# Two projections of a transformer layer in column blocks of 512 instead of 256, and a residual formed one stage earlier

## The chip, the core and the metric

The kernel runs on one core of a Trainium2 chip. The metric is the device time of one execution in microseconds (us). The core's engines work side by side, each through its own queue of instructions: TensorE (PE in the profile; its weight loads are PEld), VectorE (DVE), ScalarE (ACT), GpSimd (POOL) and SyncE (SP, which here only issues transfers). On-chip data lies in SBUF, results of TensorE in PSUM, which has eight banks of 128 x 512 fp32 here.

## What is computed

One layer of a token mixer with a feed-forward part, 1024 tokens of width 1024. Only the second half of it is touched:

```python
mix = (sigmoid(gate_a) * y_m + sigmoid(gate_b) * y_g) @ w_out      # output projection, 1024 x 1024
h = layer_norm(ALPHA * h + g1 * mix, ln1_g, ln1_b)
gate, val = split((h * (1 + sc2) + sh2) @ w_up + b_up)              # up projection, 1024 x 5632
f = (gelu(conv3x3(gate) + conv_b) * val) @ w_down + b_down          # down projection, 2816 x 1024
h = layer_norm(ALPHA * h + g2 * f, ln2_g, ln2_b)
```

The first half (two kinds of recurrent attention, their gates and their branch projections) is the same in both kernels. All is fp32. The kernel splits each operand of these products into a high and a low part (`hi` rounded to the matmul's type, `lo = x - hi`) and forms hi·hi + hi·lo + lo·hi, three matmuls for each 128 rows of the contraction.

## The kernel before

`layer_kernel` is one long function. A framework takes the instructions in program order, tracks which tiles each reads and writes, sets all waits, and may issue an instruction earlier than its place if its tiles are free; on each queue the order is then fixed, and a waiting instruction holds those behind it. Tiles with one tag share `bufs` buffers and rotate.

**Weights.** `wload` (L255) loads a piece of 2 x 128 rows by 256 columns (256 KB) through SyncE into `raw` (4 buffers), and `split` (L251) makes `hi` on ScalarE (L252) and `lo` on VectorE or GpSimd (L253), into the ring `whi`/`wlo` (6 buffers each) or into tiles given as `into`. `mm3` (L279) runs the three matmuls over all k (L283 to L285).

**SBUF places.** `slot(i)` are 16 tiles of 4 KB a partition, `ubt(i)` are 20 (`u0` to `u19`). The branch projections read slots 0 to 15 (`s` in the profile) until their last matmul, then the pool of the slots is closed and opened anew (L999 to L1001).

**Output projection** (L1041 to L1086). Token tiles 0 to 3 (`th` 0) and then 4 to 7, each in four blocks of 256 columns (`cb_`), in the order 2, 0, 1, 3 and 3, 0, 1, 2. The weights of blocks 2 and 3 go through the ring, those of 0 and 1 into slots where they stay for both halves. `mix` (L1046) loads the token tile of x once (`nt`, L1049), runs 24 matmuls of 256 columns into a `pj` bank (there are 2), multiplies by the gate row (L1055), adds ALPHA x (L1056) and takes partial statistics (L1057). In a half's last block `norm1` (L1059) normalizes the tile and stores it to DRAM as `n_d`. `mod2` (L1064) transposes four normalized tiles on TensorE, scales them on ScalarE into `u` (L1072, 3 buffers), and splits them (L1074 on VectorE, L1075 on GpSimd and VectorE in turn) into the slots that the up projection reads; the half 0 is done within the output projection, the half 1 in the first round of the up projection (L1107).

**Up projection** (L1092 to L1130). 22 rounds, each with 128 gate and 128 value columns: four groups of 24 matmuls of 512, copies out on ScalarE (L1105), a 3 x 3 convolution as eight operations on VectorE (L1120), gelu on ScalarE (L1123), the product with the value (L1124). Rounds 0 to 9 are split into `u0` to `u19` (ScalarE and GpSimd), rounds 10 to 21 are stored to DRAM as `gl_d`.

**Down projection** (L1134 to L1243). The contraction is cut in two: `g` 0 is rounds 0 to 9, `g` 1 rounds 10 to 21. For each of four blocks of 256 columns all eight token tiles have a result bank at once (`bt`: all eight banks of PSUM), and the loop takes a piece of two k at a time, all eight tiles for each. `ahead(i + 5)` keeps the ring loaded. At the end of a block VectorE forms z = result x g2 (L1201). For `g` 0 the residual is formed here: SyncE reloads `n_d` by block into `y` (L1189), VectorE multiplies and adds two rows (`gab`, `bab`, L1190 and L1191), adds z (L1203), and SyncE stores the sum to `b1_d` (L1204). During `g` 0, `reload` (L1137) brings rounds 10 to 21 back and splits them on GpSimd (L1143, L1144). Then `nt` takes the residual from `b1_d`, and for `g` 1 `evac2` (L1160) adds z and takes statistics (L1163). The last two blocks of `g` 1 run tile by tile instead (L1228), each tile 2 x 12 x 3 matmuls followed by its statistics, normalization and output store; six pieces of their weights go into other tiles (`late`, `wlate`).

Of the kernel before, what the change touches and what calls it, by code (L numbers as in the profile page):

```python
# [15 lines left out]
P = 128  # L16
# [20 lines left out]
def layer_kernel(ctx, tc, I, out, dbg=None):  # L37
# [995 lines left out]
    bst = cst.tile([P, 8, 4, 6], F32, name="bst")  # L1033
# [3 lines left out]
    def stats(t):  # L1037
# [3 lines left out]
    wo = I["w_out"]  # L1041
    wres = [([slot(4, [P, 4, 256], F32R), slot(5, [P, 4, 256], F32R)], [slot(12, [P, 4, 256], F32R), slot(13, [P, 4, 256], F32R)]),
            ([slot(6, [P, 4, 256], F32R), slot(7, [P, 4, 256], F32R)], [slot(14, [P, 4, 256], F32R), slot(15, [P, 4, 256], F32R)])]
    wb, nt, uhi, ulo = {}, {}, {}, {}

    def mix(t, cb_):  # L1046
        if t not in nt:
            nt[t] = lp.tile([P, D], F32, tag=f"n{t}", name=f"n{t}") if t < 5 else ubt(12 + t, [P, D])
            SY.dma_start(nt[t][:], x[t * P:(t + 1) * P, :])  # L1049
# [5 lines left out]
        V.tensor_tensor(m[:], p[:], g1b[:, s_], op=ALU.mult)  # L1055
        V.scalar_tensor_tensor(y, y, ALPHA, m[:], op0=ALU.mult, op1=ALU.add)  # L1056
        V.bn_stats(bst[:, t, cb_, :], y)  # L1057
# [6 lines left out]
    def mod2(th):  # L1064
        uhi[th] = [slot(4 * th + i, [P, 2, 512], F32R) for i in range(4)]
        ulo[th] = [slot(8 + 4 * th + i, [P, 2, 512], F32R) for i in range(4)]
        for k in range(KD):
# [3 lines left out]
            u = lp.tile([P, 512], F32, tag="u", name=nm("u"), bufs=3)  # L1071
# [4 lines left out]

    for th in range(2):
        for cb_ in ((2, 0, 1, 3), (3, 0, 1, 2))[th]:
            if th == 0 or cb_ == 2:
                wb[cb_] = wload([(wo, cb_ * 256, 256, 0)], into=wres[cb_] if cb_ < 2 else None)  # L1080
            for t in range(4 * th, 4 * th + 4):
                mix(t, cb_)
                if cb_ == 3 - th:
                    norm1(t)
            if th == 1 and cb_ == 3:
# [4 lines left out]
    gl_d = [drt(f"gl{f}", [P, SEQ]) for f in range(N_RES, NF)]  # L1090
    glu = {}
    for f in range(NF):  # L1092
# [7 lines left out]
        for b in range(2):  # L1100
# [23 lines left out]
        V.tensor_tensor(val[:], val[:], af, op=ALU.mult)  # L1124
        if f < N_RES:
# [9 lines left out]
    b1_d = [drt(f"b1{t}", [P, D]) for t in range(8)]  # L1135

    def reload(f):  # L1137
        t = fin.tile([P, SEQ], F32, tag="gl", name=nm("gl"), bufs=2)
        G.dma_start(t[:], gl_d[f - N_RES][:])
# [3 lines left out]
        G.tensor_scalar(hi[:], t[:], 1.0, None, op0=ALU.mult)  # L1143
        G.tensor_tensor(lo[:], t[:], hi[:].bitcast(F32), op=ALU.subtract)  # L1144
# [3 lines left out]
    todo = [(g, cb_, k) for g, (k0, k1) in enumerate(((0, N_RES), (N_RES, NF))) for cb_ in range(4)  # L1148
            for k in range(k0, k1, 2)]
    late = todo[-(NF - N_RES) // 2:]  # L1150
    wch = {}

    def prod(p, t, kk, w, first, last):
        lh, ll = (a[:, t * P:(t + 1) * P] for a in glu[kk])
        rh, rl = w(kk % 2, 0, 256)
        T.matmul(p[:], lh, rh, start=first, stop=False)  # L1156
        T.matmul(p[:], lh, rl, start=False, stop=False)  # L1157
        T.matmul(p[:], ll, rh, start=False, stop=last)  # L1158

    def evac2(t, cb_, z):  # L1160
        y = nt[t][:, cb_ * 256:cb_ * 256 + 256]
        V.tensor_tensor(y, y, z[:], op=ALU.add)
        V.bn_stats(bst[:, t, cb_, :], y)  # L1163
# [10 lines left out]
    for i, c in enumerate(todo):  # L1174
        g, cb_, k = c
        k0, k1 = ((0, N_RES), (N_RES, NF))[g]
        s_ = slice(cb_ * 256, cb_ * 256 + 256)
        if k == k0:
            acc = [pt(b, [P, 256]) for b in bt]
            if g == 0:  # L1180
                gab = fin.tile([P, 256], F32, tag="gab", name=nm("gab"), bufs=2)
                bab = fin.tile([P, 256], F32, tag="bab", name=nm("bab"), bufs=2)
                rowb(gab[:], fr_d[0:1, s_])
                rowb(bab[:], fr_d[1:2, s_])
        if g == 0 and k == k0 + 2:
            y4 = [fin.tile([P, 4, 256], F32, tag="y", name=nm("y"), bufs=2) for _ in range(2)]
            ys = [y4[t // 4][:, t % 4, :] for t in range(8)]
            for t, y in enumerate(ys):
                SY.dma_start(y, n_d[t][:, s_])  # L1189
                V.tensor_tensor(y, y, gab[:], op=ALU.mult)  # L1190
                V.tensor_tensor(y, y, bab[:], op=ALU.add)  # L1191
        if c[:2] in ((1, 2), (1, 3)):
            break
        ahead(i + 5)
        for t in range(8):
            for kk in (k, k + 1):
                prod(acc[t], t, kk, wch[c], kk == k0, kk == k1 - 1)
            if k + 2 < k1:
                continue
            z = fin.tile([P, 256], F32, tag="z", name=nm("z"), bufs=4)  # L1200
            V.tensor_tensor(z[:], acc[t][:], g2b[:, s_], op=ALU.mult)  # L1201
# [66 lines left out]
```

## Time and profile before

| | us |
|---|---|
| median of 3 runs | 2344.84 (2343.28 to 2349.64) |
| the profiled execution's own time | 2350.07 |
| its span, first to last instruction | 2348.3 |
| PE busy in it | 2265.5 (96%) |
| VectorE busy | 1363.5 (58%) |
| ScalarE busy | 719.4 (31%) |
| output projection, from 1488.9 to 1597.3 | 108.4 |
| down projection's matmuls, from 2072.4 to 2338.7 | 266.3 |

Times in the profile count from the span's start. A row of a timeline gives the start, the duration, the engine (an ending q means its queue, where a transfer is issued), the line, the operation, output and inputs, the count of merged instructions, and in brackets the idle time before it with what ended that. L283 to L285 are `mm3`'s matmuls, L1156 to L1158 those of the down projection. A matmul's row names the output bank, then the streamed operand, then the stationary one. Matmuls overlap, so a row's duration is longer than its share of time. In a group's row, count and shape come first, then busy us, mean ns, and the idle time before with what ended it.

### The profile page before, as it was taken

To read this page: it belongs to the slowest core of one execution; us is meant where nothing else is said; L and a number is where in the kernel's file an instruction comes from. 1 tells how busy PE (TensorE), PEld (TensorE's weight loads), DVE (VectorE), ACT (ScalarE), POOL (GpSimd) and SP (SyncE) were. 2 spreads that over 40 slices of the span, in tenths; PEclk is the share of its full clock that TensorE was granted. 3 is DMA by queue.
4 is the path that set the end of the run, shared out by engine and by line. 5 is a ranking of instruction groups with operands and counts; after the bars stand their busy time and mean duration, and the time that the engine had idled before them with its cause. 6 is when DMAs were issued, how large, how long until landed. Compare 5 with 4: busy or idle time off the path is not lost. (4 is left out here: it accounts for less than half of the span.)

```text
span 2348.3 us, 33481 instructions
## 1 busy us (share of the span) xinstructions
PE 2265.5 (96%) x13081; PEld 1965.0 (84%) x13081; DVE 1363.5 (58%) x2695; ACT 719.4 (31%) x1231; POOL 301.1 (13%) x254
## 2 busy tenths in 40 slices
PE   8989999998999999998999999999999999989998
PEld 4979898987889888897877788997888888889998
DVE  6484736475564645655345543577566556567457
ACT  3563323324332322313431143214333333311110
POOL 1010101111110111101210032101110000034300
PEclk9999999999999999999999999999999999999999
DMA  8222121203441333323357544512111122245511
GB/s 280 80 103 75 41 65 46 61 17 105 108 112 53 104 86 99 99 81 110 97 167 232 186 147 139 175 64 81 37 53 54 61 74 72 77 135 186 196 55 64
DMA packets 200848, 239.42 MB, mean 102 GB/s; under 512 B 16801, under 2 KB 155681, under 8 KB 200689
## 3 DMA queue, kind: packets, MB, share of 16 engines
q1 hardware_dynamic: 183521, 188.61, 25.8%
q0 software_dynamic: 8960, 31.63, 5.2%
q10 hardware_dynamic: 8208, 17.04, 2.0%
q8 instruction: 103, 1.69, 0.3%
q14 instruction: 56, 0.46, 0.1%
HBM read 183.42 MB, written 45.41 MB: 97 GB/s over the span
## 5 line engine op out<-in xcount | busy, mean ns | idle before, releaser
L252 ACT ACTIVATE whi<-raw 128x512 fp32r<-128x512 f32 x314 | 197.3, 630 | 516.1 <-PE pj L285 214.5
L283 PE MATMUL pj<-u,whi 128*128 128x512 f32 (+1 forms) x816 | 317.3, 389 | 20.3 <-DVE s L743 8.5
L253 DVE TENSOR_TENSOR wlo<-raw,whi 128x512 fp32r<-128x512 f32 x314 | 229.5, 735 | 157.5 <-ACT whi L252 153.4
L284 PE MATMUL pj<-u,whi 128*128 128x512 f32 (+1 forms) x816 | 314.3, 385 | 0.0
L285 PE MATMUL pj<-u,wlo 128*128 128x512 f32 (+1 forms) x816 | 313.8, 385 | 0.0
L283 PE MATMUL pj<-s,whi 128*128 128x512 f32 x784 | 305.6, 390 | 0.0
L285 PE MATMUL pj<-s,wlo 128*128 128x512 f32 x784 | 305.4, 390 | 0.0
L1120 DVE SCALAR_TENSOR_TENSOR acc<-g,colF,acc 128x945 f32<-128x945 f32 (+2 forms) x168 | 205.0, 1220 | 155.7 <-ACT acc L1111 153.6
L284 PE MATMUL pj<-s,whi 128*128 128x512 f32 x744 | 290.1, 390 | 2.3 <-POOL s L1075 2.3
L283 PE MATMUL pj<-whi,u 128*128 128x256 f32 x768 | 218.0, 284 | 0.0
L285 PE MATMUL pj<-whi,u 128*128 128x256 f32 x768 | 217.6, 283 | 0.0
L284 PE MATMUL pj<-wlo,u 128*128 128x256 f32 x768 | 217.6, 283 | 0.0
L283 PEld LDWEIGHTS pj<-u,whi 128*128 128x128 f32 x816 | 156.1, 191 | 51.2 <-ACT s L769 14.6
L285 PEld LDWEIGHTS pj<-u,wlo 128*128 128x128 f32 x816 | 156.0, 191 | 26.7
L284 PEld LDWEIGHTS pj<-u,whi 128*128 128x128 f32 x816 | 156.3, 192 | 25.9
L283 PEld LDWEIGHTS pj<-s,whi 128*128 128x128 f32 x784 | 147.2, 188 | 30.9
L285 PEld LDWEIGHTS pj<-s,wlo 128*128 128x128 f32 x784 | 147.2, 188 | 30.8
L284 PEld LDWEIGHTS pj<-s,whi 128*128 128x128 f32 x744 | 139.7, 188 | 33.0 <-POOL s L1075 3.6
L283 PEld LDWEIGHTS pj<-whi,u 128*128 128x128 f32 x768 | 147.4, 192 | 0.5
L284 PEld LDWEIGHTS pj<-wlo,u 128*128 128x128 f32 x768 | 147.4, 192 | 0.0
L285 PEld LDWEIGHTS pj<-whi,u 128*128 128x128 f32 x768 | 147.4, 192 | 0.0
L727 DVE SCALAR_TENSOR_TENSOR s<-pj,colB,s 128x511 f32<-128x511 f32 (+2 forms) x96 | 57.5, 613 | 92.2 <-ACT s L732 91.3
(486 smaller groups left out, 4479.8 us busy)
## 6 DMA issues: line engine op xcount, KB each, us to landing
u<-in_w_mod_dram SPq DMA_DIRECT2D x48, 512.0 KB
raw<-in_w_in_dram SPq DMA_DIRECT2D x96, 256.0 KB
raw<-in_w_up_dram SPq DMA_DIRECT2D x176, 128.0 KB
raw<-in_w_in_dram SPq DMA_DIRECT2D x96, 128.0 KB
raw<-in_w_down_dram SPq DMA_DIRECT2D x44, 256.0 KB
s<-rmask POOLq DMA_DIRECT2D x16, 512.0 KB, 5.2
s<-rr POOLq DMA_DIRECT2D x16, 512.0 KB, 7.9
qq<-re POOLq DMA_DIRECT2D x16, 512.0 KB, 6.5
```

Source lines behind the costliest of these rows:

```text
L252: A.activation(hi, src, AF.Copy)
L253: eng.tensor_tensor(lo, src, hi.bitcast(F32), op=ALU.subtract)
L283: T.matmul(p, lh, rh, start=k == 0, stop=False)
L284: T.matmul(p, lh, rl, start=False, stop=False)
L285: T.matmul(p, ll, rh, start=False, stop=k == nk - 1)
L727: V.scalar_tensor_tensor(y[:, o:o + src.shape[1]], src, t, y[:, o:o + src.shape[1]], op0=ALU.mult, op1=ALU.add)
L1120: V.scalar_tensor_tensor(av, g[:, r0 + dy:r1 + dy, c0 + dx:c1 + dx], convw(3 * ky + kx, f), av, op0=ALU.mult, op1=ALU.add)
```

## The change

Output projection: two blocks of 512 columns instead of four of 256, in the order 0, 1 and 1, 0, both blocks' weights in slots (block 0 in 4 to 7 and 12 to 15, block 1 in 0 to 3 and 8 to 11). A piece is now one k by 512 columns (`wload1`), the same 256 KB. Tiles `m` are twice as wide, `u` has two buffers instead of three, statistics have two parts a tile.

Up projection: in rounds 1 to 4, two token tiles each, GpSimd's queue loads `n_d`, VectorE multiplies and adds the two rows over all 1024 columns, and GpSimd's queue stores the result as `y_d`.

Down projection: two blocks of 512 columns, one k a step, the last two k of a block in one step per tile; eight result tiles as before. For `g` 0 only z is formed and stored to `z_d` through ScalarE's queue. The residual is put together by two transfers, `z_d` into `nt` and `y_d` added to it by an accumulating transfer on GpSimd's queue, one tile a step in the first eight steps of `g` 1. Rounds 10 to 21 are split on ScalarE and VectorE. Only the last block of `g` 1 runs tile by tile.

```diff
+    def wload1(src, c0, k, into=None):
+        raw = stg.tile([P, 512], F32, tag="raw", name=nm("raw"), bufs=4)
+        SY.dma_start(raw[:], src[k * P:(k + 1) * P, c0:c0 + 512])
+        if into is None:
+            into = [stg.tile([P, 512], F32R, tag=t, name=nm(t), bufs=6)[:] for t in ("whi", "wlo")]
+        split(into[0], into[1], raw[:], V)
+        return into
...
+    wres = {0: (4, 12), 1: (0, 8)}
...
+    def wout(cb_):
+        hs = [[slot(s0 + i, [P, 2, 512], F32R) for i in range(4)] for s0 in wres[cb_]]
+        wb[cb_] = [wload1(I["w_out"], cb_ * 512, k, [h[k // 2][:, k % 2, :] for h in hs]) for k in range(KD)]
...
-        p = pt("pj", [P, 256])
+        p = pt("pj", [P, 512])
...
-            u = lp.tile([P, 512], F32, tag="u", name=nm("u"), bufs=3)
+            u = lp.tile([P, 512], F32, tag="u", name=nm("u"), bufs=2)
...
+    wout(0)
     for th in range(2):
-        for cb_ in ((2, 0, 1, 3), (3, 0, 1, 2))[th]:
-            if th == 0 or cb_ == 2:
-                wb[cb_] = wload([(wo, cb_ * 256, 256, 0)], into=wres[cb_] if cb_ < 2 else None)
+        for cb_ in (th, 1 - th):
+            if th == 0 and cb_ == 1:
+                wout(1)
...
+        if f == 1:
+            gab, bab = ubt(16, [P, D]), ubt(17, [P, D])
+            rowb(gab[:], fr_d[0:1, :])
+            rowb(bab[:], fr_d[1:2, :])
+        if 1 <= f <= 4:
+            ys = [ubt(18 + i, [P, D]) for i in range(2)]
+            for i, y in enumerate(ys):
+                G.dma_start(y[:], n_d[2 * f - 2 + i][:])
...
+        if 1 <= f <= 4:
+            for i, y in enumerate(ys):
+                V.tensor_tensor(y[:], y[:], gab[:], op=ALU.mult)
+                V.tensor_tensor(y[:], y[:], bab[:], op=ALU.add)
+                G.dma_start(y_d[2 * f - 2 + i][:], y[:])
...
-        G.tensor_scalar(hi[:], t[:], 1.0, None, op0=ALU.mult)
-        G.tensor_tensor(lo[:], t[:], hi[:].bitcast(F32), op=ALU.subtract)
+        split(hi[:], lo[:], t[:], V)
...
-            wch[c] = wload([(I["w_down"], c[1] * 256, 256, 0)], nk=2, k0=c[2], eng=V)
+            wch[c] = wload1(I["w_down"], c[1] * 512, c[2])
...
+    loads = dict(zip((0, 2, 4, 6, 8, 10, 12, 14, 15, 16, 17, 18), range(N_RES, NF)))
+    splits = dict(zip((2, 4, 6, 8, 10, 12, 14, 16, 17, 18, 20, 21), range(N_RES, NF)))
+    main = todo[:-(NF - N_RES)]
+    for i, (g, cb_, k) in enumerate(main):
...
+            acc = [pt(b, [P, 512]) for b in bt]
+        ahead(i + 6)
+        if k == k1 - 1:
+            continue
+        ks = (k, k + 1) if k == k1 - 2 else (k,)
+        for t in range(8):
+            for kk in ks:
+                prod(acc[t], t, kk, wch[(g, cb_, kk)], kk == k0, kk == k1 - 1)
+            if len(ks) == 1:
+                continue
+            z = scaled(acc[t], s_, t % 2 if g == 0 else 0)
             if g == 0:
...
-                V.tensor_tensor(ys[t], z[:], ys[t], op=ALU.add)
-                SY.dma_start(b1_d[t][:, s_], ys[t])
-                continue
-            evac2(t, cb_, z)
+                A.dma_start(z_d[t][:, s_], z[:])
+            else:
+                evac2(t, cb_, z)
+        if i in splits:
+            gsplit(splits[i])
+        if i in loads:
+            gload(loads[i])
...
+        if i < 28:
+            t = i - 20
+            nt[t] = ubt(12 + t, [P, D])
+            SY.dma_start(nt[t][:], z_d[t][:])
+            G.dma_start(nt[t][:], y_d[t][:], accum_op=ALU.add)
...
+    for j, c in enumerate(todo[len(main):]):
+        if j >= 6:
+            if j < 10:
+                h = (ubt(10 + j - 6, [P, 2, 512], F32R) if j < 8 else
+                     fin.tile([P, 2, 512], F32R, tag="gl", name=nm("wlate"), bufs=2))
+                h = [h[:, 0, :], h[:, 1, :]]
+            else:
+                h = [fin.tile([P, 512], F32R, tag="z1", name=nm("wlate"), bufs=4)[:] for _ in range(2)]
+            wch[c] = wload1(I["w_down"], c[1] * 512, c[2], h)
+        elif c not in wch:
+            wch[c] = wload1(I["w_down"], c[1] * 512, c[2])
     for t in range(8):
-        for cb_ in (2, 3):
+        for cb_ in (1,):
...
+            evac2(t, cb_, scaled(p, slice(cb_ * 512, cb_ * 512 + 512)))
```

More of the change, by code (lines that the diff above doesn't have):

```diff
@@ L1032, in layer_kernel @@
     n_d = [drt(f"n{t}", [P, D]) for t in range(8)]
-    bst = cst.tile([P, 8, 4, 6], F32, name="bst")
+    bst = cst.tile([P, 8, 2, 6], F32, name="bst")
     mv = cst.tile([P, 8, 2], F32, name="mv")
@@ L1090, in layer_kernel @@
     gl_d = [drt(f"gl{f}", [P, SEQ]) for f in range(N_RES, NF)]
+    y_d = [drt(f"y{t}", [P, D]) for t in range(8)]
     glu = {}
@@ L1134, in layer_kernel, with gload, gsplit @@
     fin = ctx.enter_context(tc.tile_pool(name="fin", bufs=1))
[L1135 to L1139, printed above, removed]
+    z_d = [drt(f"z{t}", [P, D]) for t in range(8)]
+    gt, yt = {}, {}
+    def gload(f):
+        gt[f] = fin.tile([P, SEQ], F32, tag="gl", name=nm("gl"), bufs=2)
+        G.dma_start(gt[f][:], gl_d[f - N_RES][:])
+    def gsplit(f):
+        t = gt[f]
         i = 2 * (f - N_RES)
@@ L1154, in prod @@
         lh, ll = (a[:, t * P:(t + 1) * P] for a in glu[kk])
[L1155 to L1163, printed above, removed]
+        T.matmul(p[:], lh, w[0], start=first, stop=False)
+        T.matmul(p[:], lh, w[1], start=False, stop=False)
+        T.matmul(p[:], ll, w[0], start=False, stop=last)
     def ahead(i):
@@ L1167, in ahead, with scaled, evac2 @@
             c = todo[len(wch)]
-            wch[c] = wload([(I["w_down"], c[1] * 256, 256, 0)], nk=2, k0=c[2], eng=V)
+            wch[c] = wload1(I["w_down"], c[1] * 512, c[2])
+    def scaled(p, s_, i=0):
+        z = fin.tile([P, 512], F32, tag=f"z{i}", name=nm("z"), bufs=4)
+        V.tensor_tensor(z[:], p[:], g2b[:, s_], op=ALU.mult)
+        return z
+    def evac2(t, cb_, z):
+        y = nt[t][:, cb_ * 512:cb_ * 512 + 512]
+        V.tensor_tensor(y, y, z[:], op=ALU.add)
+        V.bn_stats(bst[:, t, cb_, :], y)
     g2b = fin.tile([P, D], F32, name="g2b")
@@ L1178, in layer_kernel @@
         if k == k0:
-            acc = [pt(b, [P, 256]) for b in bt]
-            if g == 0:
[L1181 to L1191, printed above, removed]
@@ L1207, in layer_kernel @@
-        if g == 0:
-            if i % 2 == 1 and i < 16:
-                reload(N_RES + i // 2)
-            if cb_ == 3 and k in (0, 2):
-                reload(N_RES + 8 + k)
-                reload(N_RES + 9 + k)
-            if i == 4 * (N_RES // 2) - 1:
-                lgb, lbb = ubt(8, [P, D]), ubt(9, [P, D])
-                rowb(lgb[:], I["ln2_g"].unsqueeze(0))
-                rowb(lbb[:], I["ln2_b"].unsqueeze(0))
-                for t in range(8):
-                    nt[t] = ubt(12 + t, [P, D])
-                    SY.dma_start(nt[t][:], b1_d[t][:])
@@ L1222, in layer_kernel @@
-    ahead(len(todo) - len(late))
-    for c in late:
-        j = late.index(c)
-        h = (ubt(10 + j, [P, 2, 2, 256], F32R) if j < 2 else
-             fin.tile([P, 2, 2, 256], F32R, tag=("gl", "y")[j // 2 - 1], name=nm("wlate"), bufs=2))
-        wch[c] = wload([(I["w_down"], c[1] * 256, 256, 0)], nk=2, k0=c[2], eng=V, into=([h[:, 0]], [h[:, 1]]))
+            acc = [pt(b, [P, 512]) for b in bt]
[3 more added lines that the diff above has]
+        ks = (k, k + 1) if k == k1 - 2 else (k,)
@@ L1228, in layer_kernel @@
     for t in range(8):
-        for cb_ in (2, 3):
-            bank = (2 * t + cb_) % 4
-            p = pt(("pj", "pa", "po", "pt")[bank], [P, 256])
+        for cb_ in (1,):
+            p = pt(("pj", "pa", "po", "pt")[t % 4], [P, 512])
             for kk in range(N_RES, NF):
-                prod(p, t, kk, wch[(1, cb_, kk - kk % 2)], kk == N_RES, kk == NF - 1)
-            z = fin.tile([P, 256], F32, tag="z", name=nm("z"), bufs=4)
-            V.tensor_tensor(z[:], p[:], g2b[:, cb_ * 256:cb_ * 256 + 256], op=ALU.mult)
-            evac2(t, cb_, z)
+                prod(p, t, kk, wch[(1, cb_, kk)], kk == N_RES, kk == NF - 1)
+            evac2(t, cb_, scaled(p, slice(cb_ * 512, cb_ * 512 + 512)))
```

38 lines of the change are left out of this document (13 added, 25 removed).

## Prediction

> **What bounds the kernel now.** First the page, for which engine the time belongs to, and what one matmul seems to cost; its columns are count, busy us, mean ns.
>
> ```profile
> span 2348.3 us, 33481 instructions
> ...
> L283 PE MATMUL pj<-s,whi 128*128 128x512 f32 x784 | 305.6, 390 | 0.0
> ...
> L283 PE MATMUL pj<-whi,u 128*128 128x256 f32 x768 | 218.0, 284 | 0.0
> ```
>
> The means mislead: 284 against 390 ns would make two matmuls of 256 columns 178 ns dearer than one of 512. Matmuls overlap, so what one costs is the stretch divided by the count. The table of stretches gives both (stretch; length; PE, PEld, DVE, ACT, POOL busy; granted clock; DMA share; GB/s):
>
> ```profile
> 1488.90:1597.30 108.40, 106.79 (x850) 104.70 (x850) 79.72 (x213) 20.46 (x32) 7.07 (x5) 1.00 0.38 129
> 1610.00:2072.40 462.40, 462.40 (x2041) 383.01 (x2040) 277.50 (x277) 169.28 (x226) 23.92 (x10) 1.00 0.20 61
> 2072.40:2101.50 29.10, 29.09 (x241) 28.80 (x240) 15.94 (x18) 4.80 (x7) 8.63 (x5) 1.00 0.60 189
> 2101.50:2108.80 7.30, 0.15 (x2) 0.00 (x0) 7.30 (x13) 0.63 (x1) 6.58 (x5) 0.67 0.49 144
> 2108.80:2116.00 7.20, 6.68 (x29) 6.38 (x30) 7.20 (x13) 0.00 (x0) 7.09 (x5) 0.50 0.40 127
> 2118.50:2272.00 153.50, 153.44 (x1276) 153.24 (x1277) 88.30 (x173) 20.84 (x33) 45.78 (x22) 1.00 0.49 158
> 2272.00:2338.70 66.70, 66.65 (x556) 66.44 (x554) 51.24 (x138) 0.00 (x0) 0.00 (x0) 1.00 0.15 56
> 2338.70:2348.30 9.60, 0.00 (x0) 0.00 (x0) 5.49 (x15) 0.00 (x0) 0.00 (x0) 0.72 0.15 55
> ```
>
> The up projection (1610 to 2072, all 512 wide) takes 462.4/2041 = 0.2266 us a matmul; the down projection's undisturbed end (256 wide) takes 66.7/556 = 0.120. So two narrow ones cost 0.2400 and one wide 0.2266: 13.4 ns a pair. TensorE is never idle in these stretches, so it sets the time there; PE is idle in one place only, 2101.5 to 2108.8, and at half clock after it. The timeline of PE and the chain that ended last say why:
>
> ```profile
> 1557.92 0.39 PE L283 MATMUL pj<-s,u 128*128 128x256 f32 x1 [1.61 <-DVE m L1055]
> ```
> ```profile
> 2108.83 0.58 PE L1156 MATMUL pj<-whi,u 128*128 128x256 f32 x1 [7.18 <-DVE z L1201]
> ```
> ```profile
> 2090.47 6.83 DMA y<-n
> 2097.30 2.14 DVE y L1190
> ```
>
> VectorE waited for the residual's reload, so its product z, which frees the result bank, came late.
>
> **The change, part by part.** Counts come from the loops. Output projection: 8 token tiles x 4 blocks x 24 = 768 matmuls become 384: 384 x 13.4 ns = 5.1 us. Down projection: 22 x 4 x 8 x 3 = 2112 become 1056: 14.2 us. Both lie wholly on PE, the path: **19.3 us gained**.
>
> [...]
>
> The reload's wait. 2072.4 to 2338.7 is 266.3 us; 2112 x 0.120 = 253.4; the excess is **12.9 us**, of it 7.2 us idle, 0.5 in a second gap that I leave in the sum, the rest half clock. The change takes residual work out of this stage (it is formed in rounds 1 to 4 of the up projection), and also Pool's splitting, so z is a single operation per tile; all 12.9 goes. In the output projection the 1.61 us wait (1.8 with its restart) goes too: a bank is now filled in 5.4 us instead of 2.9, so VectorE has longer. Gains together: **34.0 us**.
>
> The residual in the up projection adds two tiles x two operations a round:
>
> ```profile
> 2038.81 1.23 DVE L1124 TENSOR_TENSOR val<-val,acc 128x1024 f32<-128x1024 f32 x1 [1.19 <-ACT acc L1123]
> 2047.44 1.20 DVE L1120 SCALAR_TENSOR_TENSOR acc<-g,colF,acc 128x945 f32<-128x945 f32 x1 [7.40 <-ACT acc L1111]
> ...
> 2053.79 0.69 DVE L253 TENSOR_TENSOR wlo<-raw,whi 128x512 fp32r<-128x512 f32 x1
> ```
> ```profile
> L253 POOL TENSOR_TENSOR u<-val,u 128x1024 fp32r<-128x1024 f32 x9 | 21.5, 2393 | 173.0 <-ACT u L252 173.0
> ...
> L252 ACT ACTIVATE u<-val 128x1024 fp32r<-128x1024 f32 x9 | 9.5, 1060 | 12.1 <-DVE val L1124 12.1
> ```
> ```profile
> L1190 DVE TENSOR_TENSOR y<-y,gab x32: 410/418/3047, 2097.3 to 2182.7; 128x256 f32<-128x256 f32 x32
> ```
> ```profile
> DMA to landing us min/median/max: 3.8/4.7/9.0
> ```
>
> 4 x 1.23 = 4.9 us; between one round's product and the next convolution VectorE idles 7.40 us, which hides them. Pool's split falls into the same gap, and the y row shows an operation stretched from 0.42 to 3.05 us beside Pool; 4.9 + 2.39 = 7.3 just fits. If the cover is gone PE feels it: a round is 96 x 0.2266 = 21.75 us, round 21 starts at 2050.65 and needs the last weight difference after 19 matmuls, at 2054.95, and it ends at 2054.48. So 0.5 us is the slack. Cost 0; other end 4 x 2.4 = 9.6. The two reads and two writes a round are Pool's, where only that split waits behind them; the last row is Pool's reload of 512 KB later in the kernel, 4.7 us. The two broadcasts in round 1 stand on SyncE's queue until the second modulation has read the tiles they overwrite, some 10 us; the weight loads behind them are for round 2, 21.75 us off.
>
> The output projection's start is the first new wait. Its first block went into the ring, ahead of time; now it goes into slots that the branch projection reads until its last matmul.
>
> ```profile
> 1489.11 0.39 PE L283 MATMUL pj<-whi,u 128*128 128x256 f32 x1
> ```
> ```profile
> 1482.00 0.63 ACT L993 ACTIVATE gt<-gt 128x512 f32<-128x512 f32 x1 [2.02 <-DMA gt<-tha]
> ...
> 1489.05 1.67 ACT L252 ACTIVATE s<-raw 128x512 fp32r<-128x512 f32 x3 [2.40 <-PE pa L285]
> ...
> 1500.73 2.80 ACT L252 ACTIVATE s<-raw 128x512 fp32r<-128x512 f32 x4 [8.97 <-DMA raw<-in_w_out_dram]
> ```
> ```profile
> 1490.34 2.98 DVE L253 TENSOR_TENSOR s<-raw,s 128x512 fp32r<-128x512 f32 x3
> ...
> 1496.01 0.42 DVE L1056 SCALAR_TENSOR_TENSOR n<-n,m 128x256 f32<-128x256 f32 x1 [1.76 <-DMA n<-in_x_dram]
> ...
> 1497.45 0.42 DVE L1056 SCALAR_TENSOR_TENSOR n<-n,m 128x256 f32<-128x256 f32 x1 [0.23 <-DMA n<-in_x_dram]
> ```
> ```profile
> 1479.35 0.32 SPq L992 DMA_DIRECT2D gt<-tha  x1
> ...
> 1489.21 0.34 SPq L1049 DMA_DIRECT2D u<-in_x_dram  x1
> 1490.44 1.77 SPq L1049 DMA_DIRECT2D n<-in_x_dram  x4
> 1492.32 3.46 SPq L263 DMA_DIRECT2D raw<-in_w_out_dram  x4
> ```
>
> Slots open at 1489.05. The raw ring holds four of eight pieces; VectorE needs 1 us each from 1490.34, so these are ready by 1494.3, and piece 4 can load only when piece 0 is split. Unhindered, 256 KB land in 2.65 us (1479.35 to 1482.00): piece 7 lands at about 1497, is split at 1498.3, and the first tile ends at 1498.8 instead of 1489.11 + 24 x 0.2266 = 1494.55. Lower end 4.2 us. Upper: its loads go behind the x loads as the next block's do now (issued 1492.32, used from 1500.73), end 1504.7: 10.1, and 15.3 with the 5.2 of half clock that followed the idle stretch above (12.9 - 7.2 - 0.5). Two x loads are on SyncE's queue first in any case, and they land 1.4 us apart (the wait rows: 1496.0, then 1497.4): 4.2 + 2.8 = **7**.
>
> Second modulation, one u buffer fewer:
>
> ```profile
> 1599.82 1.27 POOL L1075 TENSOR_TENSOR s<-u,s 128x512 fp32r<-128x512 f32 x1 [41.15 <-DVE s L1074]
> ```
>
> ScalarE's third piece must now await the end of this, 1.3 us beyond its start. VectorE and Pool are already the pace, so most is hidden: **0.5**, ends 0 and 3 x 1.3 = 3.9.
>
> The last stage's weights. The ring's last two pieces (k 14 and 15 of the last block) take buffers that the merged final step reads to its end; before, one of them came free a step earlier. Behind them on VectorE's queue stand eight tiles of three operations each.
>
> ```profile
> 2265.08 0.75 DVE L1201 TENSOR_TENSOR z<-pj,g2b 128x256 f32<-128x256 f32 x2
> ...
> 2272.37 0.74 DVE L1163 BATCH_NORM_STATS2 bst<-u 128x6 f32<-128x256 f32 x2
> 2273.04 0.67 DVE L253 TENSOR_TENSOR wlo<-raw,whi 128x512 fp32r<-128x512 f32 x1
> 2273.63 1.89 DVE L253 TENSOR_TENSOR wlate<-raw,wlate 128x512 fp32r<-128x512 f32 x3
> ```
>
> Differences of 512 follow every 0.60 us (x3 in 1.89), so a tile takes 1.8 and eight 14.4, while PE fills one in 6 x 0.2266 = 1.36. VectorE starts 1.4 and ends 5.0 after PE's last; the difference is ready at 5.7, and PE needs it after 13 matmuls, at 2.95. **2.7 us**; ends 0 (differences slipped between) and 5.9 (operations not overlapped, 0.73 each), 11 with half clock.
>
> The tail:
>
> ```profile
> 2338.69 0.43 DVE z L1235
> 2339.14 0.43 DVE u L1162
> ```
>
> Three operations, 0.45 us apart at 256, 0.73 at 512: **0.8**. The rest costs nothing. Pool's twelve splits go to ScalarE (1.06) and VectorE (1.23), which in 2118 to 2272 are busy 20.84 and 88.3 of 153.5 us. Stores of z go on ScalarE's queue, each waiting for VectorE's product; behind them stand splits for pieces used five pieces of 24 x 0.2266 = 5.4 us later. The residual's eight loads and Pool's accumulating ones come three pieces, 16 us, ahead of their use; uncovered, they would delay z by the 4.7 to 9.0 us above.
>
> **Sum.** 34.0 - (7 + 0.5 + 2.7 + 0.8 = 11.0) = 23.0. The profiled execution took 2350.07 us, its span plus 1.8, and would take 2327.1. It lies 5.2 above the median of 2344.84; from the median I forecast **2321.8, say 2322**.
>
> **Rivals.**
> (a) Half clock in the new waits: the 7.3 us without matmuls were followed by 0.50. If x loads go first, the start costs 15.3 and the end 5.9: 34.0 - 22.5 = 11.5, **2333**. Against: the short waits around 1557 left their stretch at 1.00, and mine come in pieces. [...] Chance 0.21.
> (b) A wide matmul costs twice a narrow one, 0.240, where weights stream past activations (the up projection's stream the other way): the 19.3 fail, **2341**. Against: narrow ones with weights streaming run at 0.120 without a gap, so that direction has no price of its own at 256. 0.02. [...]
> (c) The change doesn't do what it says of the wait: something else delays z in the first down block and the 12.9 stay, **2335**. Against: only g2b is left to wait for, and z comes 43 us into the stage. 0.06.
> (d) Slower: the residual's multiply stands ahead of the convolution on VectorE and its load is late. Pool issues the load after its split, which ends about 2040.0 + 1.1 + 2.4 = 2043.5; landing after 4.7 to 9.0 it lets VectorE start at 2048.2 to 2052.5, end 4.9 later, and start the convolution 5.7 to 10 us late. PE then waits 5.2 to 9.5 a round, four rounds 21 to 38, and half clock 4 x 5.2 more: 42 to 59, **2364 to 2381**. It decides once the operations end over 0.5 us past 2047.4. Against: the loads can be issued a whole round ahead. 0.07.
>
> **Numbers.** Forecast 0.64. A measurement here can tell about 0.3% (7 us) from no change: 2337.8 and below is faster. All of the forecast, 0.17 of (a) and 0.05 of (c) fall there: 0.86; 0.06 of (d) slower; the rest, 0.08, the same. Best: 34.0 - 4.2 - 0.8 = 29, 2316, and 3 us less for the scatter of the runs; top: (a) with half clock at the end too, 34.0 - (15.3 + 0.5 + 11 + 0.8) = 6.4, 2338. So 2313 to 2338.
>
> **What would show it.** PE 0.2266 us a matmul in both projections; no wait in the first down block; 4 to 10 us of waits on weight differences at the output projection's start, about 3 at the last stage's; up rounds of 21.75 us throughout, 1 to 4 too. A longer round there, or clock below 1.00 at either start, makes it wrong.

## The result and the profile after

The changed kernel took 2320.1 us (median of 4 runs, 2318.58 to 2322.9) against 2344.06 (4 runs, 2342.15 to 2349.64) beside it: a ratio of 0.9895, 95% interval 0.9876 to 0.9915, or 24.0 us less. The profiled execution took 2320.08 us, span 2318.3. From the page after:

```profile
span 2318.3 us, 30341 instructions
...
PE 2241.0 (97%) x11641; PEld 1881.1 (81%) x11641; DVE 1323.9 (57%) x2511; ACT 728.3 (31%) x1239; POOL 253.9 (11%) x254
...
L285 PE MATMUL pj<-s,wlo 128*128 128x512 f32 x784 | 305.7, 390 | 2.0 <-DVE wlo L253 2.0
```

TensorE is still the bound. The spans differ by 30.0, more than the medians, because 6.3 us of it lie ahead of the first line that the change touches: the last matmul of the branch projections ends at 1488.9 before and 1482.6 after. In all profiles of this study that point lies between 1478.3 and 1488.9, so it is the scatter of one execution. I therefore compare from that point on, by stages, with a second profile of each kernel beside the first (the copies are ScalarE's of the up projection, L1105 before and L1118 after):

| from the first event to the second | before | after | change | predicted |
|---|---|---|---|---|
| last branch matmul to the first copy of round 0 (the output projection) | 103.6, 103.7 | 99.8, 99.1 | -3.8 | +0.1 |
| to its fourth copy (the second modulation lies in between) | 23.5, 23.5 | 24.8, 24.7 | +1.3 | +0.5 |
| to the last value copy of round 21 (the up projection) | 457.0, 457.0 | 460.1, 461.1 | +3.1 | 0 |
| to the end (the down stage up to the last tile's normalization, then the tail) | 275.3, 276.7 | 251.0, 249.9 | -24.3 | -23.6 |
| sum | 859.4, 860.9 | 835.7, 834.8 | -23.7 | -23.0 |

The change column takes the first profiles. Of the last row, 267.5, 268.8, 243.5 and 242.4 are the down stage, which the experiments below quote. The table of stretches after, with the columns of the prediction's table:

```profile
1482.60:1491.00 8.40, 6.13 (x25) 4.08 (x25) 5.11 (x8) 3.53 (x7) 1.52 (x1) 1.00 0.81 256
1500.00:1545.00 45.00, 45.00 (x200) 37.24 (x200) 33.94 (x78) 6.56 (x11) 0.00 (x0) 1.00 0.43 141
...
2067.30:2095.00 27.70, 27.70 (x123) 22.67 (x122) 14.27 (x15) 6.89 (x10) 2.14 (x4) 1.00 0.49 164
2095.00:2110.00 15.00, 15.00 (x68) 12.43 (x67) 7.33 (x7) 5.74 (x7) 2.50 (x5) 1.00 0.57 180
2120.00:2240.00 120.00, 120.00 (x532) 99.34 (x531) 35.19 (x51) 19.60 (x29) 7.92 (x10) 1.00 0.56 171
2258.00:2308.00 50.00, 50.00 (x222) 41.30 (x220) 40.13 (x100) 0.00 (x0) 0.00 (x0) 1.00 0.19 72
```

The first down block has neither an idle stretch nor half clock, and both projections now run at the up projection's pace: 45.00/200 = 0.2250 us a matmul in the output projection, 120.00/532 = 0.2256 and 50.00/222 = 0.2252 in the down projection. What TensorE still waits for after 1482 is the table of its waits (what waited, for what; us in total, times, longest):

```profile
PE pj L284 <- POOL s L1086: 3.0, 3, 1.5
PE pj L285 <- DVE wlo L253: 2.0, 1, 2.0
PE pj L284 <- DVE s L253: 1.3, 2, 0.7
PE pj L283 <- ACT s L252: 1.0, 2, 0.6
PE pj L1185 <- ACT wlate L252: 0.9, 1, 0.9
PE pj L283 <- ACT val L1118: 0.4, 1, 0.4
PE pj L1186 <- DVE wlate L253: 0.2, 1, 0.2
```

The same table of the kernel before:

```profile
PE pj L1156 <- DVE z L1201: 7.2, 1, 7.2
PE pj L284 <- POOL s L1075: 2.3, 3, 0.8
PE pj L283 <- DVE m L1055: 1.6, 1, 1.6
PE pa L1156 <- DVE z L1201: 0.5, 1, 0.5
```

The long wait, the one of 0.5 behind it and one of 1.6 us are gone; eleven short ones stand after it, 8.8 us together, 3.0 of them in the second modulation, where 2.3 were before. Idle time here is without the restart behind it: the 2.03 us wait at 1635.19 costs about 0.3 us more from start to start (2.75 us from 1632.78 to 1635.53, where two matmuls take 0.45).

### The profile page after: what moved, and what is told of

It is laid out like the page before. It is cut to its first block, busy times and chain, and to the rows that moved or that the text cites. A ratio compares the mean times of both kernels' runs of the same rounds, so it can differ in the third digit from the quotient of the medians.

```text
span 2318.3 us, 30341 instructions
## 1 busy us (share of the span) xinstructions
PE 2241.0 (97%) x11641; PEld 1881.1 (81%) x11641; DVE 1323.9 (57%) x2511; ACT 728.3 (31%) x1239; POOL 253.9 (11%) x254
## 4 chain that ended last, share of the span: by engine, by line
PE 76%; DMA 8%; issue 6%; DVE 6%; ACT 2%; POOL 1%; SPq 0%; DVEq 0%; POOLq 0%; ACTq 0%
PE pj L283 15%; PE pj L284 15%; PE pj L285 15%; DMA qq<-re 2%; DMA u<-in_w_mod_dram 2%; PE pa L618 2%; PE po L284 2%; PE po L283 2%; PE po L285 2%; PE pa L285 2%; PE pa L284 2%; PE pa L283 2%; DMA s<-rr 1%; PE pt L796 1%; PE po L816 1%
## 5 line engine op out<-in xcount | busy, mean ns | idle before, releaser
L253 DVE TENSOR_TENSOR wlo<-raw,whi 128x512 fp32r<-128x512 f32 x302 | 218.0, 726 | 167.2 <-ACT whi L252 163.2
L252 ACT ACTIVATE whi<-raw 128x512 fp32r<-128x512 f32 x302 | 188.8, 629 | 385.2 <-PE pj L285 155.2
L283 PE MATMUL pj<-whi,u 128*128 128x256 f32 x640 | 181.7, 284 | 0.0
L285 PE MATMUL pj<-whi,u 128*128 128x256 f32 x640 | 181.4, 283 | 0.0
L284 PE MATMUL pj<-wlo,u 128*128 128x256 f32 x640 | 181.4, 283 | 0.0
L283 PEld LDWEIGHTS pj<-whi,u 128*128 128x128 f32 x640 | 122.8, 192 | 0.5
L284 PEld LDWEIGHTS pj<-wlo,u 128*128 128x128 f32 x640 | 122.8, 192 | 0.0
L285 PEld LDWEIGHTS pj<-whi,u 128*128 128x128 f32 x640 | 122.8, 192 | 0.0
```

Source lines behind the costliest of these rows:

```text
L252: A.activation(hi, src, AF.Copy)
L253: eng.tensor_tensor(lo, src, hi.bitcast(F32), op=ALU.subtract)
L283: T.matmul(p, lh, rh, start=k == 0, stop=False)
L284: T.matmul(p, lh, rl, start=False, stop=False)
L285: T.matmul(p, ll, rh, start=False, stop=k == nk - 1)
```

## The experiments

The theory: 18 to 19 us come from the pace alone, about 13 from the end of the first down block's wait, and the rest are small new waits. The rival: the pace gives less (its limit lies elsewhere) and the residual's move gives more, or the reverse.

**How much one execution scatters.** The kernel before, once more.

> The kernel before once more, for a second profile. The profiled executions of before and after differ by 30.0 us of span, 6.3 of them ahead of the last branch matmul (1488.6 against 1482.3), where the diff touches nothing; the medians differ by 24.0. Theory: the 6.3 us are the scatter of one execution, so this profile comes to that matmul at 1479 to 1487 and takes the same 859.7 us from there to the end (within 1 us). Rival: the change made the earlier part faster (another order or other addresses), so this one comes to it at 1488.6 again.

2346.66 us, from the branch's end on 860.9 us against 859.4. The 1.5 is more than the 1 that I allowed: the first down block's long wait was 8.19 us this time instead of 7.18. It is no constant of the kernel, and stages compare to 1 to 1.5 us. The point where the branch projections end came at 1484.0, so the 6.3 us are scatter.

**The pace alone.** The changed kernel with its matmuls cut back to 256 columns, and its loads and tiles as they are:

```diff
-        mm3(p[:], lambda k: (xhi[k][:, t * P:(t + 1) * P], xlo[k][:, t * P:(t + 1) * P]), lambda k: wb[cb_][k])
+        for c in (0, 256):
+            mm3(p[:, c:c + 256], lambda k: (xhi[k][:, t * P:(t + 1) * P], xlo[k][:, t * P:(t + 1) * P]),
+                lambda k: [a[:, c:c + 256] for a in wb[cb_][k]])
...
-        T.matmul(p[:], lh, w[0], start=first, stop=False)
...
+        for j, (l, r) in enumerate(((lh, w[0]), (lh, w[1]), (ll, w[0]))):
+            if (first and j == 0) or (last and j == 2):
+                T.matmul(p[:], l, r, start=first and j == 0, stop=last and j == 2)
+                continue
+            for c in (0, 256):
+                T.matmul(p[:, c:c + 256], l, r[:, c:c + 256], start=False, stop=False)
```

> The changed kernel with every block of 512 columns, every wait and every queue as it is, but nearly all its wide matmuls (1376 of 1440) issued as two of 256 columns each into the same bank. Theory: each pair costs 13.4 ns more than the wide one, so 18.4 us more than the changed kernel's 2320.1, 2338.5, and 0.120 us a matmul in both projections. [...]

2338.82 us (6 runs), ratio 0.9975 (0.9963 to 0.9986). That is 18.7 above the changed kernel; 384 pairs in the output projection and 992 in the down projection at 13.4 ns make 18.4. The two intervals leave some 5 us either way, so by estimate a pair costs some 10 ns or more above the wide matmul (18.7 less 5 us, over 1376). Loads and tiles are the same; what differs is the count of matmuls, each of which brings its own weight load (986 of each from 2118.5 to 2240), and in the output projection the order (all of a tile's left half, then its right). That order lengthens the waits at the start from 2.3 to 4.0 us, and the waits of 1.1 us on the late pieces happened not to come, which about cancels. So the price of the narrow pair is shown for weights that stream past activations; no run here has narrow matmuls of the other direction.

**The residual alone.** The kernel before, with the residual formed in the up projection; all eight loads of `z_d` and accumulating loads of `y_d` stand at the end of `g` 0:

```diff
-                SY.dma_start(y, n_d[t][:, s_])
-                V.tensor_tensor(y, y, gab[:], op=ALU.mult)
-                V.tensor_tensor(y, y, bab[:], op=ALU.add)
...
-                V.tensor_tensor(ys[t], z[:], ys[t], op=ALU.add)
-                SY.dma_start(b1_d[t][:, s_], ys[t])
+                SY.dma_start(z_d[t][:, s_], z[:])
...
-                    SY.dma_start(nt[t][:], b1_d[t][:])
+                    SY.dma_start(nt[t][:], z_d[t][:])
+                    G.dma_start(nt[t][:], y_d[t][:], accum_op=ALU.add)
```

> The kernel before, blocks of 256 and GpSimd's splits kept, with the residual alone moved into rounds 1 to 4 of the up projection (z stored, residual added by the accumulating transfers). Theory: the wait of the first down block goes with its half clock, so the down projection's 266.3 us fall to 253.5 to 255, while the up rounds lose the 2 to 3 us that they lose in the changed kernel: about 2334. [...]

2341.24 us (10 runs), ratio 0.9991 (0.9981 to 1.0): hardly any gain, and the expected time missed by 7. The first down block has lost its wait: from 2068.4 to 2115 TensorE is busy throughout at a granted clock of 1.00, with GpSimd's splits kept and 25.45 us busy there, so they had not made z late. But the table of waits of this kernel has a new one under the same name:

```profile
PE pj L1171 <- DVE z L1204: 6.8, 1, 6.8
...
```

It lies at the end of the first block of `g` 1. The timelines of VectorE and ScalarE, and then the stretches ahead of and behind that place, tell why z is late there:

```profile
2219.37 0.69 DVE L253 TENSOR_TENSOR wlo<-raw,whi 128x512 fp32r<-128x512 f32 x1 [17.18 <-ACT whi L252]
2223.69 0.69 DVE L253 TENSOR_TENSOR wlo<-raw,whi 128x512 fp32r<-128x512 f32 x1 [3.62 <-ACT whi L252]
2224.29 0.75 DVE L1204 TENSOR_TENSOR z<-pj,g2b 128x256 f32<-128x256 f32 x2
```
```profile
2218.71 0.63 ACT L252 ACTIVATE whi<-raw 128x512 fp32r<-128x512 f32 x1 [17.25 <-DMA raw<-in_w_down_dram]
```
```profile
2190.00:2217.00 27.00, 27.00 (x227) 27.00 (x227) 2.05 (x3) 1.26 (x2) 6.04 (x7) 1.00 1.05 269
2217.00:2224.80 7.80, 1.06 (x9) 0.86 (x8) 1.81 (x4) 1.89 (x3) 0.00 (x0) 0.79 0.87 224
2224.80:2232.00 7.20, 7.14 (x46) 7.17 (x47) 7.20 (x23) 0.00 (x0) 0.00 (x0) 0.75 0.13 36
```

VectorE stood idle for 17.18 us, so it was not busy: it waited for ScalarE, and ScalarE for the next weight piece. The next two pieces, issued on SyncE's queue behind its eight loads of `z_d` while GpSimd's queue issued the eight accumulating ones, had not landed (DMA share 1.05 at 269 GB/s), and their differences stand ahead of z on VectorE's queue. The name in this wait's row is the last in a queue, not the cause. The changed kernel issues one tile a step over eight steps, and has no such wait.

**The residual alone, loads reordered.** To see whether the order of that burst decides:

```diff
-                    SY.dma_start(nt[t][:], z_d[t][:])
-                    G.dma_start(nt[t][:], y_d[t][:], accum_op=ALU.add)
+                for c0, c1 in ((0, 256), (256, 1024)):
+                    for t in range(8):
+                        SY.dma_start(nt[t][:, c0:c1], z_d[t][:, c0:c1])
+                        G.dma_start(nt[t][:, c0:c1], y_d[t][:, c0:c1], accum_op=ALU.add)
```

> The residual-only kernel once more, but its eight loads and eight accumulating loads are issued for the first 256 columns of every tile ahead of those for the other 768. Theory (the 12.9 us belong to whatever makes the product z late, and the first block of the second half waited in the residual-only kernel only because every tile had to be complete in all its columns): no PE gap above 2 us in the down projection, no half clock in it, stage from the last product to the last tile 254.5 to 257.5 us instead of 263.7 and 267.5, time 2332 to 2336, ratio 0.995 to 0.9965. Rival (the accumulating loads are themselves too slow when issued together, whatever their order, or the weight load behind them is what is late): a gap of 4 to 8 us near 2225 with half clock after it, stage above 261, time 2339 to 2343.

2337.55 us (12 runs), ratio 0.997 (0.996 to 0.9981); the down stage took 259.2 us, a value between the two accounts. VectorE's timeline again:

```profile
2216.06 0.69 DVE L253 TENSOR_TENSOR wlo<-raw,whi 128x512 fp32r<-128x512 f32 x1 [3.66 <-ACT whi L252]
2216.67 0.75 DVE L1204 TENSOR_TENSOR z<-pj,g2b 128x256 f32<-128x256 f32 x2
```

A wait of 2.24 us for z is left, again right behind a late weight piece; three more of 0.3 follow. So my theory of that experiment (only completeness of the tiles matters) fell, and its rival holds at a third of its size: the weight load behind the burst is what is late. The down stage is 8.3 us below the first profile of before and 9.6 below the second, with 3.0 of waits in it: that is 11.3 to 12.6 for the first block's wait, close to the 12.9. And the up projection took 459.0 instead of 457.0 in this kernel (459.2 in the one before), which its expectation had left out.

**The output projection alone.** The kernel before with the wide blocks of the output projection, two `u` buffers and nothing else of the change:

```diff
-        for cb_ in ((2, 0, 1, 3), (3, 0, 1, 2))[th]:
+        for cb_ in (th, 1 - th):
...
-            u = lp.tile([P, 512], F32, tag="u", name=nm("u"), bufs=3)
+            u = lp.tile([P, 512], F32, tag="u", name=nm("u"), bufs=2)
...
```

> The kernel before with the output projection alone in blocks of 512 (with its two u buffers), everything after it as before. Theory: 5.1 us by the pace and 1.8 by the wait at the second modulation, against 3.4 at the start and 0.8 to 1.3 at the second modulation's end: the stretch from the last branch matmul to the second round is 2 to 3 us shorter, 2341 to 2342. Rival: the new waits eat it all, 2344 or more.

2339.88 us (10 runs), ratio 0.9977 (0.9965 to 0.9989). Its stage is 100.0 us, 3.6 below before, and the modulation 24.1 (+0.6), together 3.0 less, as expected; the up projection takes 457.0. The 3.1 us that the changed kernel loses in the up projection thus belong to the residual's work there.

**GpSimd's splits.** The changed kernel with the splits of rounds 0 to 4 on VectorE:

```diff
-            split(hi[:], lo[:], val[:])
+            split(hi[:], lo[:], val[:], V if f < 5 else G)
```

> The changed kernel with the low parts of rounds 0 to 4 formed on VectorE instead of GpSimd. In the changed kernel PE waits 2.2 us in round 1 (1632.8 to 1635.2) for a weight difference, behind a residual operation that took 3.43 instead of 1.23 us while GpSimd split, and 0.5 in round 2. Theory: GpSimd's split holds VectorE up, so the 2.2 us go, though VectorE does 1.2 us more a round; the up projection takes 457 to 458 us instead of 460.1 from the fourth to the last copy. Rival: the loads of the residual are late (1.73 and 0.82 us waits on them stand in front of the convolution), so the wait stays or grows.

2314.76 us (4 runs), ratio 0.9872 (0.9856 to 0.9887), the up projection 457.1 us. VectorE in the changed kernel, and GpSimd beside it:

```profile
1628.85 1.20 DVE L1142 SCALAR_TENSOR_TENSOR acc<-g,colF,acc 128x945 f32<-128x945 f32 x1 [0.40 <-ACT acc L1133]
1629.97 3.43 DVE L1149 TENSOR_TENSOR u<-u,u 128x1024 f32<-128x1024 f32 x1
1633.33 1.21 DVE L1142 SCALAR_TENSOR_TENSOR acc<-g,colF,acc 128x960 f32<-128x960 f32 x1
1634.45 0.68 DVE L253 TENSOR_TENSOR wlo<-raw,whi 128x512 fp32r<-128x512 f32 x1
```
```profile
1629.91 2.40 POOL L253 TENSOR_TENSOR u<-u,u 128x1024 fp32r<-128x1024 f32 x1 [2.53 <-ACT u L252]
```

The same place in this experiment:

```profile
1627.57 1.22 DVE L253 TENSOR_TENSOR u<-u,u 128x1024 fp32r<-128x1024 f32 x1
1628.70 1.22 DVE L1142 SCALAR_TENSOR_TENSOR acc<-g,colF,acc 128x960 f32<-128x960 f32 x1
1629.83 0.69 DVE L253 TENSOR_TENSOR wlo<-raw,whi 128x512 fp32r<-128x512 f32 x1
```

The residual's multiplication takes 3.43 us beside GpSimd's split instead of 1.23, the weight difference behind it is 2 us late, and TensorE waits for that. With the split on VectorE itself, 1.22 us, all waits of the up projection are gone, while VectorE's waits for the residual's loads stay (1.68 and 0.87 us, against 1.73 and 0.82): the loads are not the cause, GpSimd's split beside VectorE is. The edit also moves the multiplication to a later place on VectorE's queue, and how much of the 3.0 us that alone would give back was not tried. The 3.43 us are nearly 2.40 + 1.23, the split's time and the multiplication's own. The delay shows the other way round too: in the next round GpSimd's split starts at 1650.22, 0.07 us behind a residual addition, and this time the split is the one that takes long, 3.42 us, and the addition 1.23.

**The start of the output projection.** The changed kernel with the first six pieces of block 0 in the ring, loaded again into their slots for the second half:

```diff
-        wb[cb_] = [wload1(I["w_out"], cb_ * 512, k, [h[k // 2][:, k % 2, :] for h in hs]) for k in range(KD)]
+        wb[cb_] = [wload1(I["w_out"], cb_ * 512, k, None if cb_ == 0 and k < 6 else [h[k // 2][:, k % 2, :] for h in hs])
+                   for k in range(KD)]
...
```

> The changed kernel with the first six weight pieces of output block 0 in the ring, as the block before was, and loaded a second time into the slots for the second half. Theory: the 3.4 us of waits at the output projection's start are those of the slots, so 3 or more of them go. Rival: the x loads and the splits set the start, so half or more of the wait stays.

2319.17 us (4 runs), ratio 0.989 (0.9871 to 0.9909). The waits at the start are gone, but the stage takes 98.6 us, 1.2 less than in the first profile of the changed kernel and not 3.4. Six other profiles of kernels with the old start have 99.1 to 100.2, so 0.5 to 1.6 is all that can be claimed: four waits of 0.2 us each, with their restarts, came up some 25 us later on block 1's pieces, which now load behind six more.

**The u buffers.** The changed kernel with three `u` buffers and one of `m`:

```diff
-        m = lp.tile([P, 512], F32, tag="m", name=nm("m"), bufs=2)
+        m = lp.tile([P, 512], F32, tag="m", name=nm("m"), bufs=1)
...
-            u = lp.tile([P, 512], F32, tag="u", name=nm("u"), bufs=2)
+            u = lp.tile([P, 512], F32, tag="u", name=nm("u"), bufs=3)
```

> The changed kernel with three u buffers again and, to make room, one m buffer, which VectorE alone writes and reads. Theory: the second modulation's end loses 0.8 to 1.3 us by the missing buffer, which come back, 23.5 us instead of 24.8 from the first to the fourth copy of round 0. Rival: the residual's operations of round 1, which VectorE takes in between there, make the loss, and it stays.

2313.8 us (4 runs), ratio 0.9868 (0.9849 to 0.9886). The modulation is back at 23.5 us, so the 1.3 goes with the third buffer. Two buffers without the residual cost 0.6 (the output projection alone, above); the other half needs the residual's operations beside them. The rest of the run's gain isn't its doing: the wait on the late pieces happened not to come (down stage 242.1), the up projection took 459.1, and the branch projections ended at 1479.9.

**The late pieces.** The changed kernel with the last two ring pieces loaded after the six that go elsewhere:

```diff
-    for j, c in enumerate(todo[len(main):]):
+    last = todo[len(main):]
+    for j, c in sorted(enumerate(last), key=lambda a: (a[0] in (4, 5), a[0])):
```

> The changed kernel with the last stage's six pieces that have free places loaded ahead of the two that wait for the ring. In the changed kernel PE waits 1.6 us there, for the eleventh piece's load (ACT wlate 0.88, DVE wlate 0.22). Theory: the raw buffers held by the two waiting pieces keep that load back, so with the order turned the 1.6 us go, and nothing replaces them. Rival (the step of the prediction): the two ring pieces' differences are what is late, so 1 to 3 us appear at them.

2320.68 us (4 runs), ratio 0.9897 (0.9881 to 0.9913). The wait at 2253 is gone, but it is gone as well in two kernels that left this order alone, and the whole is no faster. Inconclusive: it depends on when a load lands.

**The edits together.** First the splits, the buffers and the late order at once; then the ring for the start as well; and the changed kernel again beside them.

> The changed kernel with three edits that were each run alone: GpSimd's splits of rounds 0 to 4 moved to VectorE, a third u buffer, the late pieces in the other order. Theory (they remove three separate waits, so they add): 3.0 + 1.3 + 0 to 1.6 below the changed kernel's 2320.1, so 2314.2 to 2315.8; up projection 457 us, second modulation 23.5, down stage about 242. Rival (the waits share their cover, and one that goes leaves the next): 2317 or more, with the up projection or the down stage back at the changed kernel's 460 or 243.5.

> As the kernel with three edits, and the first six pieces of the output projection's first block go to the ring first. Theory (only 1.2 of the 3.4 us of waits at the start went with this edit alone): output projection 98.6 us, 1.2 us below the three edits, 2312.5 to 2315. Rival (the stage is held up by VectorE's splits, which are doubled for six pieces): the same time as the three edits within 0.5 us or above it.

> The changed kernel itself again, beside the three above on one chip: 2318 to 2322, from the start of the output projection to the span's end 835 to 837 us.

| kernel | median us | ratio (95%) | from the branch's end, us |
|---|---|---|---|
| changed, again | 2318.61 | 0.9889 (0.9873 to 0.9906) | 834.8 |
| three edits | 2314.36 | 0.9865 (0.9845 to 0.9885) | 830.0 |
| four edits | 2312.48 | 0.9867 (0.9849 to 0.9885) | 829.1 |

Four runs each. The three edits add as expected: modulation 23.5, up projection 457.0, down stage 241.9. They take 4.8 us off the stages; the intervals of the ratios still overlap, also with those of the splits alone and of the buffer alone. The fourth edit takes 0.8 us off its stage, which lies within that stage's scatter, and cannot be told from none.

## Why the prediction was right, and which steps were not

The mechanism of the two large terms was right, and the total came within 2 us. That it came so close is partly luck: the start, the last ring pieces and the tail were costed 6.7 us too high, and the up projection, the second modulation and a wait on a late piece (1.1 us, 1.7 with its restarts), which I had not foreseen, some 5.6 us too low. Of my signs, the pace and the first down block came as said; 4 to 10 us at the start and about 3 at the last stage did not, and round 1 of the up projection was longer, which I had named as a sign against me.

- **Pace, 19.3 us**: right. The narrow matmuls measure 18.7 us for 1376 pairs; the rival in which a wide matmul costs twice a narrow one is out.
- **The first down block's wait, 12.9 us**: right in the changed kernel; the residual alone, with its loads reordered, gives 11.3 to 12.6 there. But "only g2b is left to wait for" was not the whole of it. z waits for what stands ahead of it on VectorE too, and where the new loads are issued in a burst, a wait of 6.8 us comes back at another place. That the change spreads them over eight steps is, by these runs, what made my step hold (the changed kernel with a burst was not run); I had weighed only whether the loads come in time themselves.
- **The start of the output projection, 7 us**: 3.4 us from start to start, below my lower end of 4.2. The pieces were late much as I had said, but the step from there to the cost failed. SyncE's queue of the changed kernel, then ScalarE, then VectorE's first operation on each tile's product:

```profile
1482.91 0.33 SPq L1060 DMA_DIRECT2D u<-in_x_dram  x1
1484.25 0.33 SPq L1060 DMA_DIRECT2D n<-in_x_dram  x1
1484.81 3.23 SPq L1044 DMA_DIRECT2D raw<-in_w_out_dram  x4
1488.09 1.38 SPq L1060 DMA_DIRECT2D n<-in_x_dram  x3
```
```profile
1482.75 1.67 ACT L252 ACTIVATE s<-raw 128x512 fp32r<-128x512 f32 x3 [3.43 <-PE pa L285]
...
1490.14 1.96 ACT L252 ACTIVATE s<-raw 128x512 fp32r<-128x512 f32 x3 [4.68 <-DMA raw<-in_w_out_dram]
```
```profile
1494.80 0.69 DVE L1066 TENSOR_TENSOR m<-pj,u 128x512 f32<-128x512 f32 x1 [0.96 <-PE pj L285]
1497.30 0.69 DVE L1066 TENSOR_TENSOR m<-pj,u 128x512 f32<-128x512 f32 x1 [0.35 <-PE pj L285]
```

  Two x loads did go first, and four weight loads stand ahead of the other three. The first tile's product was taken at 1494.80; by estimate, 24 matmuls back to back from 1482.8 would have ended near 1488.4 (24 x 0.2266 and the last one's overlap), so that tile was about 6.4 us late, nearly my 7. But the second tile's product follows 2.50 us behind it, where 24 matmuls take 5.44: on TensorE's queue the second tile's matmuls stand among the first's, so TensorE worked on while the first tile waited. I had counted the first tile's delay as TensorE's loss.
- **The second modulation, 0.5 us**: 1.3 and 1.2, inside my ends; a GpSimd subtraction stretched from 1.27 to 2.27 us beside a residual multiplication made the largest of its waits 1.5, and with a third `u` buffer the stretch was gone and the largest wait was 0.8, as before the change.
- **The up projection, 0 us**: this step failed. It measured 3.1 and 4.1 us. I took the 7.40 us in which VectorE idled before for the place where the residual's operations go. They stand between the convolution's operations instead, all sixteen from 1597.8 to 1651.4, before the end of round 2, and one ran beside GpSimd's split, in front of a weight difference with 0.5 us of slack. I had the stretching and the slack, and summed them over a free gap, not along the queue. The other end, 9.6, was too high, because only one of four rounds was hit in full.
- **The last ring pieces, 2.7 us**: not there, though VectorE was as late as I had worked out. VectorE's queue, then TensorE's:

```profile
2245.11 0.68 DVE L1201 TENSOR_TENSOR u<-u,z 128x512 f32<-128x512 f32 x1
2245.70 0.69 DVE L253 TENSOR_TENSOR wlo<-raw,whi 128x512 fp32r<-128x512 f32 x1
```
```profile
2244.05 0.39 PE L1185 MATMUL pa<-whi,s 128*128 128x512 f32 x1
...
2246.55 0.39 PE L1187 MATMUL pa<-whi,s 128*128 128x512 f32 x1
2246.78 0.39 PE L1186 MATMUL pj<-wlo,s 128*128 128x512 f32 x1
```

  The first difference stands behind 23 of the 24 operations and ends at 2246.39; the first tile (bank `pj`) could have used it from 2244.05. But TensorE's queue holds twelve matmuls of the second tile (`pa`) just there, 12 x 0.2266 = 2.7 us, and takes the difference at 2246.78; three more stand ahead of the next one. So the wait was covered, not by VectorE, as my end of 0 had it, but by TensorE's own order, as at the start. A wait of 0.9 and 0.2 us on a late piece stood nearby, by a raw load and not by this mechanism.
- **The tail, 0.8 us**: the three operations are 0.73 apart as predicted:

```profile
2308.29 0.69 DVE L1196 TENSOR_TENSOR z<-pt,g2b 128x512 f32<-128x512 f32 x1 [1.53 <-PE pt L1187]
2309.01 0.69 DVE L1201 TENSOR_TENSOR u<-u,z 128x512 f32<-128x512 f32 x1
2309.74 0.69 DVE L1202 BATCH_NORM_STATS2 bst<-u 128x6 f32<-128x512 f32 x1
```

  From z to the end are 10.0 us instead of 9.6, so 0.4.
- **The rivals.** Half clock in the new waits (a) did not come at the two starts; it came, small, in the up projection (below). (c) did not happen here, but its point, that something else can delay z, is what the residual alone showed. (b) is out by the narrow matmuls. (d) had the right place and wrong size: a multiplication does get ahead of a convolution's operation, but only one round pays for it, and GpSimd's split makes it late, not its load.

Not placed: some 0.7 us of the down stage, and what decides whether the late piece's wait comes.

## What to carry to other kernels

Cost a matmul by stretch over count, never by the mean of its rows, and a change of width by that difference. Before counting an idle gap as cover, ask where in the engine's queue the new operations will land, what stands behind them with how much slack, and which engine works beside them. Before counting a late tile as TensorE's loss, ask which other matmuls stand there on its queue. And when work moves out of a late stage, its transfers come back somewhere: issue them one at a time, and look for the weight load that falls behind them.

## What the chip showed that I had not expected

Short waits can bring half clock, and equal waits don't always. In the changed kernel's first profile the 2.03 us wait at 1635.19 left the clock at 1.00. In its second, one of 2.25 us at the same matmul brought half clock: matmuls came 0.43 us apart from 1635.2 to 1638.6, which costs about 1.6 us. The same wait was 2.19 us with narrow matmuls, 2.17 with the ring at the start and 2.90 with the late order, each with half clock behind it; the 2.24 us with the residual by block had none.

So the length alone does not decide. What goes with it can be read from the traces: in the first profiles of both kernels the clock changes only at points that lie whole multiples of 3.413 us apart (the stretches of half clock that end within the span are 3.413, 6.827 or 13.653 us long; the half clock after the 2.25 us lasts from 1635.15 to 1638.57, that of the kernel before from 2104.00 to 2117.66, four times as long). Cut into these windows, the places above look like this, first the second profile of the changed kernel, then its first (the second number is TensorE's busy time):

```profile
1631.74:1635.15 3.41, 1.22 (x5) 1.05 (x6) 3.41 (x5) 0.00 (x0) 0.00 (x0) 1.00 0.48 163
1635.15:1638.57 3.42, 3.42 (x9) 2.64 (x9) 3.42 (x5) 0.69 (x1) 0.00 (x0) 0.50 0.42 117
```
```profile
1630.23:1633.64 3.41, 2.93 (x13) 2.08 (x12) 3.41 (x2) 1.67 (x4) 2.58 (x2) 1.00 0.29 85
1633.64:1637.05 3.41, 1.86 (x8) 1.55 (x9) 3.41 (x5) 0.63 (x1) 0.00 (x0) 1.00 0.65 197
```

The 2.25 us fell into one window almost whole, 2.19 us of it, and the next window ran at half clock; the 2.03 us were cut by an edge into 0.48 and 1.55. In the kernel before, the 7.18 us wait put 2.35 us into the window from 2100.59 to 2104.00, and half clock followed; the 1.61 us wait put 1.55 into the one from 1554.45 to 1557.86, and the clock stayed at 1.00. Of the 2.19 us with narrow matmuls some 1.95 lay, by estimate from where its half clock begins (1644.44), in the window ahead of it. From 1478 us to the last matmul, the first profiles of both kernels have no window at full clock with more idle time than those 1.55 us that wasn't followed by half. That holds for this stretch; earlier in the program, with other matmuls, the two overlap (in the kernel before half clock from 537.28 on, after 1.25 us, and none from 701.13 on, after 1.80).
